# Four lo buffers, two pairs of buffers in turns for the activations, and an earlier last gate piece in layer 0

## The chip, the cores and the metric

The kernel runs on one core of one Trainium2 chip. Its time is the device time of one execution in microseconds (us). The core's engines are TensorE (PE in the profile; its weight loads are PEld), VectorE (DVE), ScalarE (ACT), GpSimd (POOL, almost unused here) and SyncE (SP), which issues the loads of the weights.

## What is computed

One launch computes two transformer blocks of two layers each, on one sequence of 256 tokens with 1024 features, in float32. Cut to what matters:

```python
def first_block(...):                 # layers 0 and 1
    for l in range(DEPTH):
        sh1, sc1, gt1, sh2, sc2, gt2 = split(silu(c) @ w_ada[l] + b_ada[l], 6)
        u = x * (1 + sc1) + sh1
        y = mixer(u, ...)
        x = layer_norm(DN_ALPHA * x + (1 + gt1) * y, ...)
        u = x * (1 + sc2) + sh2
        h = square(relu(u @ w_up[l])) @ w_down[l]
        x = layer_norm(DN_ALPHA * x + (1 + gt2) * h, ...)

def mixer(u, ...):
    q, k, v, glu_in, g_attn, g_conv = split(u @ w_in)
    y_attn = moba_attention(q, k, v) @ w_attn_br
    h = a * sigmoid(g)                # the two halves of glu_in
    h = silu(layer_norm(depthwise_conv31(h) + dw_b, ln_g, ln_b))
    y_conv = h @ w_pw
    return (sigmoid(g_attn) * y_attn + sigmoid(g_conv) * y_conv) @ w_out

def second_block(...):                # layers 2 and 3
    for l in range(DEPTH):
        h = rmsnorm(x, ...)           # three attentions ya, yb, yc from h @ w_in
        gates = sigmoid(h @ w_gate[l] + b_gate[l])
        merged = sum(gates[b] * (y[b] @ w_br[b]))
        x = x + merged @ w_o[l]
        h = rmsnorm(x, ...)
        x = x + (silu(h @ w_ffn_gate[l]) * (h @ w_ffn_up[l])) @ w_ffn_down[l]
    return rmsnorm(x, final_norm_g)
```

## The kernel before

**Weights.** All weights are streamed once, in pieces of 128 x 2048 float32 (1 MB), in the order of a list (`weight_order`). `fetch` (L126 to L141) loads a piece into one of three `raw` buffers by a DMA on SP's queue (L131), ACT casts it to `whi` (L138, in two halves of 128 x 1024, four buffers) and DVE subtracts to get the rest `wlo` (L139, two halves, three buffers). Activations are split in the same way by `split` (L149 to L151: ACT the high part, DVE the low one). A product takes three matmuls: high by high, low weight by high activation, high weight by low activation. So a piece is ready when both halves of its `wlo` are written, and a `wlo` buffer comes free when the last matmul that reads it is done.

**Order.** On PE the instructions stand in the order of the program. DVE, ACT and SP get theirs from a list scheduler when the kernel is built, which also takes the number of buffers into account; each engine then works through its list in order. Small side work (the condition's projection at L374, L419, L421 and L439, attention, convolution) is put between the pieces by `tick`.

**Handovers.** Between a mixer and a feed-forward part, and between two layers, `handover` (L671) orders PE, DVE and ACT by hand. It runs the last matmuls of the output projection (L206 to L208), adds the residual, normalises each of the two halves of 128 tokens (DVE, L761 to L778 for LayerNorm; L841, L845 and L883 for RMS norm; L866 to L877 for the LayerNorm that is followed by an RMS norm), transposes the result on PE (L732), writes the new activation `u` (LayerNorm: DVE L794, ACT L801, DVE L803 and L808; RMS norm: L905, L907) and starts the next projection (L222, L223, L228) before the second half is normalised. There are eight of them: three with LayerNorm, one with both norms (block 1 to block 2), three with RMS norm and the last at the end of the kernel. `later` holds back the splits of pieces that are fetched afterwards until the handover's last instructions; splits of pieces fetched before it may be placed by the scheduler anywhere ahead or inside.

**Buffers of activations.** `u` (high and low, 16 KB a partition) has one buffer, pool `u2`. A pool `s8` of four 8 KB buffers holds `xT` at the start, the two gates `gt` and the merged result `mg` of `mixer1`, and in block 2 `n_`, `kTc`, two of the three `gt` and `mg`.

**Layer 0's mixer.** `mixer1` computes q, k, v and the gates from `w_in`. The depthwise convolution is 30 taps on DVE (L952), spread over the mixer. Its output is transposed on PE by the first `next(cl)` (L967), normalised on DVE (L969, `moments`, L972), transposed back (L332, second `next(cl)`), passed through silu (L982, L983, L985) and split into `hc` (L150, L151), which the convolution's branch, `branch(1, hc, c, merge)`, multiplies by its weights. Around these steps stand the attention's branch in two pieces, `branch(0, y, 0)` and `branch(0, y, 1)`, and the last piece of the gates, `gates(1, [3])`:

```python
        self.finish(conv)
        ...
        next(cl)
        branch(0, y, 0, None)
        next(cl)
        branch(0, y, 1, None)
        gates(1, [3])
        ...
        for c in range(2):
            branch(1, hc, c, merge)
```

**Feed-forward of block 1.** `ffn1` takes the pieces of `w_up` and `w_down` in turns: an up piece (L175, L177), evacuated by ACT (L188) and DVE (L189), squared, split, and multiplied by a down piece (L206 to L208).

Of the kernel before, what the change touches and what calls it, by code (L numbers as in the profile page):

```python
# [9 lines left out]
F32 = mybir.dt.float32  # L10
F32R = mybir.dt.float32r
# [5 lines left out]
P = 128  # L17
D = 1024
S = 256
KT = D // P  # L20
# [44 lines left out]
class Net:  # L65
    def __init__(self, ctx, tc, ins, out, stop=None, dump=None):
        self.tc, self.nc, self.i, self.out = tc, tc.nc, ins, out
        self.stop, self.dumps = stop, dump or {}
        self.uid = 0
        self.pools = {}  # L70
        for name, bufs in (("raw", 3), ("whi", 4), ("wlo", 3), ("s8", 4), ("u2", 1), ("s4", 7), ("b4", 2), ("one", 1), ("sm", 3)):
            self.pool(ctx, name, bufs)
        self.pool(ctx, "ps", 8, space=PSUM)
        self.pool(ctx, "dr", 1, space=bass.MemoryType.DRAM)
        self.queue = weight_order(ins)
        self.ready = []
        self.tracks = []
        self.behind = []
        self.ada = {}
# [268 lines left out]
    def new_u(self):  # L348

        t = self.t("u2", [P, 2, KT, S], F32R)  # L350
        return t[:, 0], t[:, 1], t

    def new_fm(self, n=KT, pool="s8"):
        return self.t(pool, [P, n, S], F32R), self.t(pool, [P, n, S], F32R)
# [175 lines left out]
    def start(self):  # L530


        nc, i = self.nc, self.i
# [8 lines left out]
        a, n = PC["b_ada"]  # L542
        self.par1 = self.t("one", [P, n], tag="par1")
        nc.vector.tensor_scalar(self.par1, self.par[:, a:a + n], 1.0, None, op0=ALU.add)
        u = self.new_u()
        xT = self.t("s8", [P, KT, S])
        A, B = self.ada_cols(0, 1), self.ada_cols(0, 0)
# [3 lines left out]
        a, n = CC["cmask"]  # L551
# [438 lines left out]
    def mixer1(self, l, u, ps):  # L990
        nc, i = self.nc, self.i
        first = l == 0
# [56 lines left out]
        def qkf(h):  # L1049
            r = slice(64 * (h % 2), 64 * (h % 2) + 64)  # L1050
            return qT[r, h // 2, :], kT[r, h // 2, :]
        gt = [self.t("s8", [P, KT, S]) for _ in range(2)]

# [34 lines left out]
        hc = self.new_fm(4, "s4")  # L1088
        cl = self.conv_ln(l, cv, hc)
        next(cl)  # L1090
        branch(0, y, 0, None)
        next(cl)
        branch(0, y, 1, None)
        gates(1, [3])
        self.finish(ada)
        self.dump(f"hc{l}", hc[0].bitcast(F32))
        mg = self.new_fm()

# [110 lines left out]
    def mixer2(self, l, u, ps):  # L1209
# [3 lines left out]
        pcs = [[p for _, p in ps], [p for _, p in self.as_512(u)]]  # L1213
        n_ = self.new_fm()
        mn = self.mla_norm(pcs, gq, n_)
# [63 lines left out]
        qTc = self.t("s8x", [P, 8, S])  # L1279
        kTc = self.t("s8", [P, 8, S])  # L1280
        for src, dst in ((qcs, qTc), (kcs, kTc)):
# [41 lines left out]

        gt = [self.t("s8x" if b == 1 else "s8", [P, KT, S]) for b in range(3)]
        bh = self.small(24, "bgh")
        nc.vector.tensor_scalar(bh, self.par_("b_gate", l * 24, 24), 0.5, None, op0=ALU.mult)
        for b in (2, 0, 1):
            for c in range(4):
                w = self.w()
                for m in range(2):  # L1330
# [4 lines left out]
                    nc.scalar.activation(g, g, AF.Tanh, scale=0.5, bias=bh[:, b * 8 + k:b * 8 + k + 1])  # L1335
        mg = self.new_fm()
        for b in (2, 0, 1):
# [125 lines left out]
def weight_order(i):  # L1463

    o = []
    for l in range(L):
        w = i["w_in_a" if l == 0 else "w_in_b"]
        o += [w[c] for c in range(w.shape[0])]
        last = o.pop()
        o += [i["w_attn_br"][l, c] for c in range(2)] + [last]  # L1470
        for name in ("w_conv_pw", "w_out"):
            o += [i[name][l, c] for c in range(i[name].shape[1])]
        o += [i["w_up"][l, c] for c in range(3)]
        for c in range(3, 19):
            if c < 16:
                o.append(i["w_up"][l, c])
            o.append(i["w_down"][l, c - 3])
# [18 lines left out]
def build(tc, ins, out, stop=None, dump=None):  # L1496
    with ExitStack() as ctx:
# [6 lines left out]
        if stop is None or stop.startswith("2"):  # L1504
            with ExitStack() as c2:
                for name, bufs in (("bias", 3), ("s8x", 1)):
                    net.pool(c2, name, bufs)
                net.block2()
# [149 lines left out]
```

## Time and profile before

| What | Value |
|---|---|
| Runs | 1732.88, 1733.07, 1734.87 us, median 1733.07 |
| Profiled execution | 1733.14 us, of it span of the trace 1731.2 |
| Busy: PE, DVE, ACT | 1661.8, 1281.8, 958.8 us (96, 74, 55%) |
| Share of the chain that ended last | PE 89%, DVE 7%, DMA 2%, ACT 1% |
| Granted TensorE clock, mean | 0.989 of full speed |

The profile is of one execution. PE is busy for nearly the whole span, so time can be taken only out of the stretches in which PE waits, and out of those in which its clock is granted at half (1.2 instead of 2.4 GHz, written 0.50). The views below show where these are: who let PE wait and how long, the chain of work that ended last in order of time, the instructions of one engine in a stretch, and the granted clock in stretches.

### The profile page before, as it was taken

The page shows a single profiled execution, that of the slowest core. Times are in us where ns is not written, and L with a number is a line of the kernel's source. Part 1 is how long each engine was busy: PE and PEld are TensorE (multiplying, and loading weights), DVE is VectorE, ACT ScalarE, POOL GpSimd, SP SyncE. Part 2 cuts the span into 40 slices and gives each one's busy share as a digit, 9 for nine tenths or more (in the row PEclk, how much of TensorE's full clock was granted, in tenths as well). Part 3 has the DMA queues.
Part 4 walks back from the last instruction along what each step waited for, and adds up shares of the span by engine and source line. Part 5 has one row for each costly group of instructions (what it writes and reads, how often), then busy time and mean ns, then how long its engine had stood idle before and what let it go on. Part 6 is the DMA issues. An engine that isn't in the chain of part 4 may idle for free.

```text
span 1731.2 us, 25828 instructions
## 1 busy us (share of the span) xinstructions
PE 1661.8 (96%) x10008; PEld 1436.9 (83%) x10008; DVE 1281.8 (74%) x2497; ACT 958.8 (55%) x1750; POOL 2.6 (0%) x12
## 2 busy tenths in 40 slices
PE   6998999998999999997999999999999999999998
PEld 5887888787888888885988898888889888988887
DVE  7999788578997886557856677766676566876665
ACT  3564375464355375553566754655455677455553
POOL 0000000000000000000000000000000000000000
PEclk9999999999999999998999999999999999999999
DMA  8884568584874466653544444555545444445551
GB/s 337 342 318 173 199 223 316 196 294 176 308 247 182 171 229 233 219 192 140 208 152 150 147 151 179 195 195 195 191 150 203 149 147 146 164 168 198 182 190 72
DMA packets 59974, 347.37 MB, mean 201 GB/s; under 512 B 6558, under 2 KB 10700, under 8 KB 25676
## 3 DMA queue, kind: packets, MB, share of 16 engines
q1 hardware_dynamic: 59852, 345.73, 55.3%
q8 instruction: 78, 1.28, 0.3%
q14 instruction: 44, 0.36, 0.1%
HBM read 344.63 MB, written 2.64 MB: 201 GB/s over the span
## 4 chain that ended last, share of the span: by engine, by line
PE 89%; DVE 7%; DMA 2%; ACT 1%; issue 0%; SPq 0%; DVEq 0%; ACTq 0%
PE ps L175 23%; PE ps L177 12%; PE ps L207 8%; PE ps L206 8%; PE ps L208 8%; PE ps L160 5%; PE ps L161 5%; PE ps L164 4%; PE ps L228 3%; PE ps L222 3%; PE ps L223 2%; DVE wlo L139 2%; PE ps L439 1%; PE ps L332 1%; PE ps L487 1%; PE ps L464 1%
## 5 line engine op out<-in xcount | busy, mean ns | idle before, releaser
L139 DVE TENSOR_TENSOR wlo<-raw,whi 128x1024 fp32r<-128x1024 f32 (+1 forms) x534 | 629.7, 1211 | 206.3 <-PE ps L177 104.0
L138 ACT CAST whi<-raw 128x1024 fp32r<-128x1024 f32 (+1 forms) x534 | 534.1, 1043 | 279.4 <-PE ps L208 80.6
L175 PE MATMUL ps<-u,whi 128*128 128x512 f32 x1728 | 438.9, 396 | 0.0
L175 PEld LDWEIGHTS ps<-u,whi 128*128 128x128 f32 x1728 | 313.9, 188 | 65.3 <-issue 5.7
L206 PE MATMUL ps<-whi,s 128*128 128x512 f32 (+2 forms) x688 | 253.6, 369 | 3.8 <-ACT whi L138 3.8
L207 PE MATMUL ps<-wlo,s 128*128 128x512 f32 (+2 forms) x688 | 253.0, 368 | 0.5 <-DVE wlo L139 0.5
L208 PE MATMUL ps<-whi,s 128*128 128x512 f32 (+2 forms) x688 | 252.3, 367 | 0.0
L177 PEld LDWEIGHTS ps<-u,wlo 128*128 128x128 f32 x1728 | 235.6, 190 | 17.2
L177 PE MATMUL ps<-u,wlo 128*128 128x256 f32 x1728 | 240.7, 282 | 0.0
L206 PEld LDWEIGHTS ps<-whi,s 128*128 128x128 f32 x688 | 130.3, 189 | 23.9 <-ACT whi L138 4.0
L208 PEld LDWEIGHTS ps<-whi,s 128*128 128x128 f32 x688 | 130.0, 189 | 21.0 <-DVE s L151 0.7
L207 PEld LDWEIGHTS ps<-wlo,s 128*128 128x128 f32 x688 | 130.2, 189 | 19.8 <-DVE wlo L139 1.2
L222 PE MATMUL ps<-whi,u 128*128 128x512 f32 x240 | 98.2, 409 | 11.0 <-ACT u L801 10.9
L188 ACT COPY ev<-ps 128x256 f32<-128x256 f32 x136 | 50.2, 369 | 92.1 <-PE ps L177 92.1
L952 DVE SCALAR_TENSOR_TENSOR s<-s,dw,s 128x255 f32<-128x255 f32 (+17 forms) x240 | 96.2, 462 | 0.0
L223 PE MATMUL ps<-wlo,u 128*128 128x512 f32 x240 | 96.0, 400 | 0.0
L160 PE MATMUL ps<-u,whi 128*128 128x256 f32 x352 | 89.4, 292 | 0.2 <-DVE s L941 0.2
L161 PE MATMUL ps<-u,whi 128*128 128x256 f32 x352 | 85.9, 282 | 0.0
L160 PE MATMUL ps<-s,whi 128*128 128x256 f32 x320 | 82.4, 289 | 0.0
L161 PE MATMUL ps<-s,whi 128*128 128x256 f32 x320 | 81.0, 285 | 0.3 <-DVE s L151 0.3
L189 DVE TENSOR_TENSOR ev<-ps,ev 128x256 f32<-128x256 f32 x136 | 56.8, 420 | 28.9 <-ACT ev L188 28.1
L151 DVE TENSOR_TENSOR s<-ev,s 128x256 fp32r<-128x256 f32 (+1 forms) x72 | 39.1, 542 | 48.9 <-PE ps L207 37.7
(263 smaller groups left out, 2123.2 us busy)
## 6 DMA issues: line engine op xcount, KB each, us to landing
raw<-in_w_fgu_dram SPq DMA_DIRECT2D x44, 1024.0 KB, 4.8
raw<-in_w_up_dram SPq DMA_DIRECT2D x32, 1024.0 KB, 5.0
raw<-in_w_down_dram SPq DMA_DIRECT2D x32, 1024.0 KB, 5.6
raw<-in_w_in_dram SPq DMA_DIRECT2D x32, 1024.0 KB, 4.8
ada<-in_w_ada_p_dram SPq DMA_DIRECT2D x48, 512.0 KB, 5.1
raw<-in_w_gate_dram SPq DMA_DIRECT2D x24, 1024.0 KB, 4.8
raw<-in_w_fd_dram SPq DMA_DIRECT2D x22, 1024.0 KB, 4.8
raw<-in_w_in_b_dram SPq DMA_DIRECT2D x18, 1024.0 KB, 6.1
```

Source lines behind the costliest of these rows:

```text
L138: nc.scalar.copy(hi[:, a:b], raw[:, a:b])
L139: nc.vector.tensor_sub(lo[:, a:b], raw[:, a:b], hi[:, a:b].bitcast(F32))
L160: mm(ps, whi[:, b], ahi[:, k, :], start=j == 0, stop=False)
L161: mm(ps, whi[:, b], alo[:, k, :], start=False, stop=False)
L175: mm(p2, whi[:, (blk + k) * P:(blk + k + 1) * P], both[:, :, k, :], start=k == 0, stop=False)
L177: mm(p[:, :S], wlo[:, (blk + k) * P:(blk + k + 1) * P], uhi[:, k, :], start=False, stop=k == KT - 1)
L206: mm(ps, ahi[:, k, tok], whi[:, cols], start=first, stop=False, **grp)
L207: mm(ps, ahi[:, k, tok], wlo[:, cols], start=False, stop=False, **grp)
L208: mm(ps, alo[:, k, tok], whi[:, cols], start=False, stop=last, **grp)
L222: mm(p, ahi[:, k, tok], whi[:, cols], start=k == 0, stop=False)
L223: mm(p, ahi[:, k, tok], wlo[:, cols], start=False, stop=False)
L952: nc.vector.scalar_tensor_tensor(cv[:, ct, d:], hp[:, ct, :S - d], wk, cv[:, ct, d:], op0=ALU.mult, op1=ALU.add)
```

## The change

It has three parts.

1. Pool `wlo` gets four buffers instead of three.
2. To make room, pool `s8` goes. Pool `u2` now holds two buffers of 16 KB by the names `ua` and `ub`. `new_u` takes them in turns; `xT`, `gt`, `mg` and `n_` are halves of one or both. In block 2 `s8x` gets a second buffer, for `kTc`.
3. In layer 0 alone, `gates(1, [3])` is written ahead of the first `next(cl)`, and `weight_order` lists its weight piece ahead of the two pieces of `w_attn_br`. Layer 1 keeps its order.

```diff
-        for name, bufs in (("raw", 3), ("whi", 4), ("wlo", 3), ("s8", 4), ("u2", 1), ("s4", 7), ("b4", 2), ("one", 1), ("sm", 3)):
+        for name, bufs in (("raw", 3), ("whi", 4), ("wlo", 4), ("u2", 1), ("s4", 7), ("b4", 2), ("one", 1), ("sm", 3)):
...
     def new_u(self):
-        t = self.t("u2", [P, 2, KT, S], F32R)
+        self.turn = not self.turn
+        t = self.pair("ua" if self.turn else "ub", F32R)
         return t[:, 0], t[:, 1], t
+    def pair(self, tag, dt=F32):
+        return self.t("u2", [P, 2, KT, S], dt, tag=tag)
...
-        xT = self.t("s8", [P, KT, S])
+        xT = self.pair("ub")[:, 0]
...
-        gt = [self.t("s8", [P, KT, S]) for _ in range(2)]
+        gt = self.pair("ub")
+        gt = [gt[:, b] for b in range(2)]
...
         cl = self.conv_ln(l, cv, hc)
+        if first:
+            gates(1, [3])
         next(cl)
         branch(0, y, 0, None)
         next(cl)
         branch(0, y, 1, None)
-        gates(1, [3])
+        if not first:
+            gates(1, [3])
...
-        mg = self.new_fm()
+        mg = self.pair("ua", F32R)
+        mg = mg[:, 0], mg[:, 1]
...
-        n_ = self.new_fm()
+        n_ = self.pair("ub", F32R)
+        n_ = n_[:, 0], n_[:, 1]
...
-        gt = [self.t("s8x" if b == 1 else "s8", [P, KT, S]) for b in range(3)]
+        gt = self.pair("ub")
+        gt = [gt[:, 0], self.t("s8x", [P, KT, S]), gt[:, 1]]
...
-        o += [i["w_attn_br"][l, c] for c in range(2)] + [last]
+        br = [i["w_attn_br"][l, c] for c in range(2)]
+        o += br + [last] if l else [last] + br
...
-                for name, bufs in (("bias", 3), ("s8x", 1)):
+                for name, bufs in (("bias", 3), ("s8x", 2)):
```

No instruction is added or taken away. The order of the instructions changes at the following places, among others. In the listings a row is line, operation, output, inputs and size; line numbers in the changed kernel are larger (L139 becomes L140, L761 L767, L794 L800, L967 L973, L969 L975), and numbers behind a name count buffers.

DVE in the first handover, before (`ps_2074` holds the projection's result for the second half of the tokens, `ps_2262` the transposed first half; L794 starts the new `u`):

```order
L778 TENSOR_SCALAR x_119<-x_119,mv_2242,r_r_2250 128x512
L761 TENSOR_TENSOR ev_2287<-ps_2074,G_263_1683 128x512
L765 SCALAR_TENSOR_TENSOR x_119<-x_119,ev_2287 128x512
L768 BN_STATS bn_346_2286<-x_119 128x6
L139 TENSOR_TENSOR wlo_2151<-raw_2148,whi_2150 128x1024 x2
L794 TENSOR_SCALAR ev_2284<-ps_2262,pl_a_2161,pl_b_2162 128x128 x2
```

The same place after:

```order
L784 TENSOR_SCALAR x_116<-x_116,mv_2237,r_r_2245 128x512
L767 TENSOR_TENSOR ev_2282<-ps_2069,G_238_1637 128x512
L771 SCALAR_TENSOR_TENSOR x_116<-x_116,ev_2282 128x512
L774 BN_STATS bn_344_2281<-x_116 128x6
L800 TENSOR_SCALAR ev_2279<-ps_2257,pl_a_2156,pl_b_2157 128x128 x2
```

And after, ahead of the handover's first DVE instruction (L767; before, `wlo_2143` stood last ahead of it, and `wlo_2143` of before is `wlo_2138` here, `wlo_2151` is `wlo_2146`):

```order
L152 TENSOR_TENSOR ua_1934<-ub_744,ua_1934 128x512
L140 TENSOR_TENSOR wlo_2138<-raw_2135,whi_2137 128x1024 x2
L140 TENSOR_TENSOR wlo_2146<-raw_2143,whi_2145 128x1024 x2
L767 TENSOR_TENSOR ev_2200<-ps_2067,G_238_1637 128x512
L771 SCALAR_TENSOR_TENSOR x_116<-x_116,ev_2200 128x512
```

The two halves of L139 have moved from inside the handover to the place right ahead of it. The same is found in the next six handovers; the last has none in either kernel.

ACT in the feed-forward of layer 0, before (`ps_3275` and `ps_3302` hold an up piece's result, `whi_3229` is the down piece that PE uses next, `whi_3268` the up piece behind it):

```order
L188 COPY ev_3274<-ps_3275 128x256
L188 COPY ev_3274<-ps_3302 128x256
L1118 ACTIVATE ev_3274<-ev_3274 128x512
L1119 ACTIVATE ev_3274<-ev_3274 128x512
L150 CAST s_517_3323<-ev_3274 128x512
L138 CAST whi_3229<-raw_3227 128x1024 x2
L138 CAST whi_3268<-raw_3266 128x1024 x2
```

After (`whi_3224` is `whi_3229` of before, `whi_3263` is `whi_3268`):

```order
L151 CAST s_484_3122<-ev_3078 128x512
L139 CAST whi_3224<-raw_3222 128x1024 x2
L189 COPY ev_3169<-ps_3170 128x256
L189 COPY ev_3169<-ps_3197 128x256
L1129 ACTIVATE ev_3169<-ev_3169 128x512
L1130 ACTIVATE ev_3169<-ev_3169 128x512
L151 CAST s_499_3218<-ev_3169 128x512
L189 COPY ev_3269<-ps_3270 128x256
L189 COPY ev_3269<-ps_3297 128x256
L1129 ACTIVATE ev_3269<-ev_3269 128x512
L1130 ACTIVATE ev_3269<-ev_3269 128x512
L151 CAST s_515_3318<-ev_3269 128x512
```

The cast of the down piece has moved two up pieces ahead; that of the up piece behind it still follows L151 of `s_515_3318`. DVE's subtractions moved with them: the down piece's stands two up pieces earlier, and that of the up piece behind it (`wlo_3264`) now follows three instructions of side work (L425, L427, L380).

PE in layer 0's mixer, before (`ev_1519` and `ev_1525` are attention's, `s_59_499` the convolution's output, `ps_1670` the attention's branch):

```order
L510 MATMUL ps_1471<-ev_1519,s_57_497 64x128
L510 MATMUL ps_1471<-ev_1525,s_57_497 64x128
L967 MATMUL ps_1612<-con_118,s_59_499 128x128 x4
L967 MATMUL ps_1637<-con_118,s_59_499 128x128 x4
L160 MATMUL ps_1670<-s_102_745,whi_1301 128x256
```

After, the end of the last gate piece (`ps_1612`) and what follows it:

```order
L162 MATMUL ps_1612<-ua_103,whi_1297 128x256
L165 MATMUL ps_1612<-ua_103,wlo_1298 128x256 x8
L445 MATMUL ps_1670<-ada_1642,c_sel_486 32x256 x4
L445 MATMUL ps_1670<-ada_1644,c_sel_486 32x256 x4
L973 MATMUL ps_1686<-con_115,s_59_496 128x128 x4
L973 MATMUL ps_1711<-con_115,s_59_496 128x128 x4
L161 MATMUL ps_1744<-s_102_742,whi_1424 128x256
```

The gate piece now lies between attention's last matmul and the transposes of the convolution's output. DVE behind the convolution, before, from the last tap on:

```order
L952 SCALAR_TENSOR_TENSOR s_59_499<-s_58_498,dw_500,s_59_499 128x226 x2
L139 TENSOR_TENSOR wlo_1665<-raw_1662,whi_1664 128x1024
L969 BN_STATS bn_238_1617<-ps_1612 128x6
L969 BN_STATS bn_249_1642<-ps_1637 128x6
L322 BN_AGGR mv_1619<-bn_238_1617 128x2
L139 TENSOR_TENSOR wlo_1665<-raw_1662,whi_1664 128x1024
L304 TENSOR_SCALAR r_x_1621<-mv_1619 128x1
```

The same place after:

```order
L958 SCALAR_TENSOR_TENSOR s_59_496<-s_58_495,dw_497,s_59_496 128x226 x2
L140 TENSOR_TENSOR wlo_1607<-raw_1604,whi_1606 128x1024 x2
L425 TENSOR_TENSOR G_238_1637<-ps_1638,b_222_1459 128x256
L975 BN_STATS bn_247_1691<-ps_1686 128x6
L427 TENSOR_SCALAR G_238_1637<-G_238_1637 128x256
L323 BN_AGGR mv_1693<-bn_247_1691 128x2
L975 BN_STATS bn_258_1716<-ps_1711 128x6
L305 TENSOR_SCALAR r_x_1695<-mv_1693 128x1
L140 TENSOR_TENSOR wlo_1739<-raw_1736,whi_1738 128x1024
L305 TENSOR_SCALAR r_y_1696<-r_x_1695 128x1
L323 BN_AGGR mv_1718<-bn_258_1716 128x2
L140 TENSOR_TENSOR wlo_1739<-raw_1736,whi_1738 128x1024
```

Four halves of `wlo` and one pair of L425 and L427 now stand ahead of the first normalised half (L972, now L978) where two halves did. From the last tap to the last split of `hc` (L151, now L152) it is seven halves, where it was four.

## Rows read from the trace of the kernel before

**Rows 1.** Waits of PE: line, releaser, us in total, times, longest us.

```profile
PE ps L732 <- DVE s L883: 18.0, 8, 8.3
...
PE ps L222 <- ACT u L801: 10.9, 6, 3.0
PE ps L967 <- DVE s L952: 5.8, 1, 5.8
```

**Rows 2.** The chain that ended last, in order of time: start, us, what.

```profile
210.64 2.36 DVE wlo L139 x2
235.43 1.85 PE ps L175 x8
...
1535.76 2.36 DVE wlo L139 x2
```

**Rows 3.** Timeline of DVE in the first handover: start, us, instruction, idle before it.

```profile
210.64 2.36 DVE L139 TENSOR_TENSOR wlo<-raw,whi 128x1024 fp32r<-128x1024 f32 x2
...
219.02 0.54 DVE L778 TENSOR_SCALAR x<-x,mv,r_r 128x512 f32<-128x512 f32 x1
```

**Rows 4.** Timeline of PE in the first handover.

```profile
214.40 0.50 PE L222 MATMUL ps<-whi,u 128*128 128x512 f32 x1 [3.02 <-ACT u L801]
...
220.67 0.60 PE L732 MATMUL ps<-con,x 128*128 128x128 f32 x4
```

**Rows 5.** Stretches: length, busy by engine, PEclk (granted clock), DMA share, GB/s.

```profile
216.00:217.00 1.00, 1.00 (x4) 0.81 (x3) 0.93 (x4) 0.41 (x1) 0.00 (x0) 0.50 0.95 401
...
411.00:413.00 2.00, 1.97 (x9) 1.63 (x10) 1.99 (x5) 1.97 (x5) 0.00 (x0) 1.00 0.93 352
```

**Rows 6.** Timeline of DVE, then of PE, in the first RMS handover.

```profile
1073.23 2.36 DVE L139 TENSOR_TENSOR wlo<-raw,whi 128x1024 fp32r<-128x1024 f32 x2 [1.25 <-PE ps L207]
...
1080.79 0.30 PE L732 MATMUL ps<-con,s 128*128 128x128 f32 x1 [1.75 <-DVE s L883]
```

**Rows 7.** Timeline of ACT, then of DVE, at the start of the first handover.

```profile
198.11 2.00 ACT L138 CAST whi<-raw 128x1024 fp32r<-128x1024 f32 x2 [3.44 <-PE ps L208]
...
200.79 0.69 DVE L761 TENSOR_TENSOR ev<-ps,G 128x512 f32<-128x512 f32 x1 [0.53 <-PE ps L208]
...
203.66 0.42 DVE L761 TENSOR_TENSOR ev<-ps,G 128x256 f32<-128x256 f32 x1 [0.67 <-PE ps L208]
```

**Rows 8.** Layer 0's feed-forward: timelines of PE, ACT, DVE, and a stretch.

```profile
336.18 0.80 PE L206 MATMUL ps<-whi,s 128*128 128x512 f32 x1 [3.84 <-ACT whi L138]
...
335.08 5.78 ACT L138 CAST whi<-raw 128x1024 fp32r<-128x1024 f32 x6
...
329.90 0.41 DVE L419 TENSOR_TENSOR G<-ps,b 128x256 f32<-128x256 f32 x1
330.35 0.29 DVE L421 TENSOR_SCALAR G<-G 128x256 f32<-128x256 f32 x1
...
338.43 1.28 DVE L374 CUSTOM_DVE_ANT_0 ada<-ada,c_row,par 128x1024 f32<-128x1024 f32 x1
...
338.00:340.00 2.00, 2.00 (x6) 1.54 (x5) 2.00 (x4) 2.00 (x4) 0.00 (x0) 0.50 0.00 0
```

**Rows 9.** Layer 0's mixer: timelines of PE and DVE, and a stretch.

```profile
149.49 1.27 PE L967 MATMUL ps<-con,s 128*128 128x128 f32 x4 [5.81 <-DVE s L952]
...
167.89 0.47 PE L160 MATMUL ps<-u,whi 128*128 128x256 f32 x1
...
175.26 0.47 PE L160 MATMUL ps<-s,whi 128*128 128x256 f32 x1
...
155.63 0.80 DVE L972 TENSOR_SCALAR ev<-ps,mv,r_r 128x512 f32<-128x512 f32 x1
...
169.29 0.69 DVE L151 TENSOR_TENSOR s<-ev,s 128x512 fp32r<-128x512 f32 x1
...
150.00:152.00 2.00, 2.00 (x10) 2.00 (x11) 2.00 (x3) 0.00 (x0) 0.00 (x0) 0.50 0.04 8
```

**Rows 10.** The page's groups: line, engine, operation, count, busy, mean ns, idle before.

```profile
L189 DVE TENSOR_TENSOR ev<-ps,ev 128x256 f32<-128x256 f32 x136 | 56.8, 420 | 28.9 <-ACT ev L188 28.1
```

More of the change, by code (lines that the diff above doesn't have):

```diff
@@ L77, in __init__ @@
         self.tracks = []
+        self.turn = False
         self.behind = []
@@ L348, in new_u, with new_fm @@
     def new_u(self):
-        t = self.t("u2", [P, 2, KT, S], F32R)
+        self.turn = not self.turn
+        t = self.pair("ua" if self.turn else "ub", F32R)
         return t[:, 0], t[:, 1], t
-    def new_fm(self, n=KT, pool="s8"):
+    def pair(self, tag, dt=F32):
+        return self.t("u2", [P, 2, KT, S], dt, tag=tag)
+    def new_fm(self, n, pool):
         return self.t(pool, [P, n, S], F32R), self.t(pool, [P, n, S], F32R)
@@ L1279, in mixer2 @@
         qTc = self.t("s8x", [P, 8, S])
-        kTc = self.t("s8", [P, 8, S])
+        kTc = self.t("s8x", [P, 8, S])
         for src, dst in ((qcs, qTc), (kcs, kTc)):
@@ L1335, in mixer2 @@
                     nc.scalar.activation(g, g, AF.Tanh, scale=0.5, bias=bh[:, b * 8 + k:b * 8 + k + 1])
-        mg = self.new_fm()
+        mg = self.pair("ua", F32R)
+        mg = mg[:, 0], mg[:, 1]
         for b in (2, 0, 1):
```

## Prediction

> **What bounds the kernel now.** PE is busy for 96% of the span (the table), so I read first who lets it wait. In the waits of PE [rows 1] three of the long ones matter here: the transposes of the normalised halves wait for DVE (L732 for L883: 18.0 us in eight waits, the longest 8.3), the first projection of a handover waits for ACT's `u` (L222: 10.9 us in six, the longest 3.0), and in layer 0 the transposes of the convolution's output wait 5.8 us for its last taps (L967). Then I look for what keeps the releaser. In the chain in order of time "DVE wlo L139 x2" stands seven times within a handover, at 210.64, 407.27, 598.25, 783.44, 1073.23, 1261.18 and 1535.76, each 2.35 or 2.36 us (the first and the last are in [rows 2]). The timeline of DVE shows the first of them between the residual work and the step that makes `u` [rows 3]. These two halves belong to a weight piece that nothing in the handover reads. With three `wlo` buffers, two are held by the last pieces of the output projection and one by the next piece, so the split has to wait until one comes free, and that is inside the handover.
>
> **Part 1, the fourth lo buffer: handovers.** In the order of after both halves stand ahead of the handover, seven times. What returns is read from the wait that ends last in each.
>
> First handover. L222 starts at 214.40 after a wait of 3.02 [rows 4]; its input comes from DVE through L794 and ACT, right behind the two halves, so 2.36 come back. The wait shrinks to 0.7. There is more: behind the long wait the clock was granted at 0.50 for three us (one of them in rows 5), half speed, in which up to 1.5 are lost. The second transposes start at 220.67 [rows 4], while `x` was ready at 219.02 + 0.54 = 219.56 [rows 3], so at most 1.1 of that can be regained before DVE is the limit. I take 0.8: 3.2 in all, bounds 2.4 and 3.5.
>
> A row and a rule differ a little here. After the same wait of 3.0 in the second handover the clock stayed at 1.00 (411 to 413 in [rows 5]). The Trainium skill (TensorE: Matmul & The Clock Gate, Part 1, What's actually happening) says that the clock falls to half after an idle stretch and that the window that is watched runs free of the program; by this, equal waits can cost clock in one place and none in another, and the traces agree (0.50 after one, 1.00 after the other). By the rule the 0.8 might stay lost here or turn up elsewhere, and the sum would be 0.8 smaller. That case is a rival below.
>
> Second and third handover: same waits, no clock loss, and DVE carries the chain to the second transposes as well: 2.36 each. Fourth, with both norms: PE waits for DVE throughout (8.3 at its longest [rows 1]), so DVE's 2.35 is the gain. Fifth to seventh (RMS): the second transposes wait 1.75 for L883 (the first of them, at 1080.79, is in [rows 6]), which lies behind the two halves on DVE. This wait goes whole; beyond it PE's own work is the limit, except for a small gap that L905 (also behind the halves) leaves. So between 1.75 and 2.36, and I take 2.0 each. Sum: 3.2 + 4.7 + 2.4 + 6.0 = **16.3**, bounds 14.0 (5.2 for the last three, 2.4 for the first, 0.1 lost in each as below) and 17.7.
>
> What the moved halves now stand in front of: L761, the handover's first DVE step. Their cast still needs a `whi` buffer that PE frees at 198.1 (ACT, 198.11 to 200.11 [rows 7]). The low half follows its cast, so the last ends near 200.11 + 1.2 = 201.3 to 201.5, and L761, at 200.79 before [rows 7], starts 0.6 or 0.7 later. The cover is DVE's idle time of 0.67 ahead of the next L761 at 203.66 [rows 7]. So I cost it at nothing (up to 0.1 each); without that cover it would be 0.7 each.
>
> **Part 1, feed-forward of layer 0.** At 336.18 PE waits 3.84 for a cast of a down piece, which ACT did in a run of six halves from 335.08, after a long time without any [rows 8]. In the order of after this cast and its subtraction stand two up pieces earlier, so the wait goes. Behind it the clock was at half (0.50 in 338 to 340 [rows 8]): from 336.18 to 341 I estimate 4 to 5 us at half speed, which lose about 2.2. Against this stands a new wait. The subtraction of the next up piece (`wlo_3264`) now stands on DVE behind L425, L427 and L380, which are L419, L421 and L374 of before: 0.41 + 0.29 + 1.28 [rows 8]. They start when PE's ones-matmul (L418) is done, right ahead of the up piece; with the first half of the subtraction (1.18) PE's low matmuls can start 3.2 after that, and PE gets there after eight high ones, 1.85 [rows 2]. So PE waits about 1.3. Sum 3.84 + 2.2 - 1.3 = **4.7**; bounds 2.5 (no clock regained) and 6.0 (no new wait). Elsewhere in the order I find no other split with so little room.
>
> **Part 2, the buffers.** Counts and sizes stay. `mg` in `ua` may be written once the last gate piece has read `u`; on PE that piece lies ahead of the branch whose result `mg` holds. The next `u` in `ub` comes after the merge's last read. No queue gets a new wait, cost nothing. If that were wrong the place is the first merge of each mixer.
>
> **Part 3, the earlier gate piece.** It takes PE from 167.89 to 175.26, 7.4 us [rows 9], and fills the wait of 5.81 ahead of L967 at 149.49 [rows 9]. Behind that wait the clock was 0.50 (150 to 152 [rows 9]): 1.0 is lost in these two us, and I estimate as much again for the us on either side, some 1.9. By PE alone, then, 5.81 + 1.9 = 7.7 could come back, the upper bound. But DVE is next. Its last split of `hc` ends at 169.29 + 0.69 = 169.98 [rows 9], and the last tap does not move. In the order of after, seven halves of L140 instead of four stand in between, 3 x 1.18 = 3.5 more. Of the first transposed half (L972, at 155.63 [rows 9]) PE's transposes back will have to wait some 2.5, where PE had its own work before. I take it that one of the three halves falls into time in which DVE waits anyway: `hc` ends near 172.3. The convolution's branch then starts near 172.3 instead of 175.26 [rows 9]: **3.0**. Lower bound 0, if DVE's chain slips by another 3. Its SP loads and casts move with the piece and were early there.
>
> **Sum.** 16.3 + 4.7 + 3.0 = 24.0. The profiled execution took 1733.14, 0.07 above the median of the runs (1733.07), so nothing is corrected: 1733.1 - 24.0 = **1709.1**. Bounds: 14.0 + 2.5 + 0 = 16.5 gives 1716.6; 17.7 + 6.0 + 7.7 = 31.4 gives 1701.7.
>
> **Rivals.**
> 1. *Layer 0's move gives nothing.* DVE's chain from the last tap to `hc` takes all that PE gains. For it: three more halves in that chain, and the taps end when they did. Against: `hc` had 5.3 us of room (169.98 to 175.26), and three halves are 3.5. Time 1733.1 - 21.0 = 1712.1.
> 2. *The moved halves hold up the handover's start.* Decides when the cast ends over 0.1 later than I read it: the cover is 0.67, used to 0.6. If the whole 2.36 is paid ahead of L761 in the three LayerNorm handovers and the fourth, 4 x 2.36 = 9.4 of the gain is lost: 1718.5. Against: PE's release of the buffer at 198.1 doesn't depend on the change.
> 3. *The clock stays low where I have it return*, after the waits that are left in the first handover (0.7) and the feed-forward (1.3): 0.8 + 2.2 lost, 1712.1. Against: the long waits that went before the low clock are gone.
> 4. *The pairs add a wait*, and the change doesn't do what it says: a merge that waits for the last reader of `u` in each of four layers, 6 us each, ends at 1733. Against: the order on PE.
> 5. *Slower.* Earlier splits stand in DVE's in-order list ahead of evacuations of PSUM (L189, 136 of them [rows 10]) and wait there for their cast, so that PE finds no free bank. The idle time ahead of L189 is 28.9 / 136 = 0.21 each [rows 10]; from a new PE wait of 24.0 / 136 = 0.18 each the gain is gone, at 0.25 the time is 1709.1 + 34.0 = 1743.1. Against: the waits of PE name L189 nowhere, so PSUM has had slack.
>
> **How the numbers follow.** Forecast (all three parts within their bounds, 1702 to 1716): 0.58. Rival 1: 0.14, rival 2: 0.12, rival 3: 0.10, rival 4: 0.03, rival 5: 0.03. The first three end within 1709 to 1719, so the range is 1701 to 1719, and 0.06 of the cases and some tails lie outside it. Within 0.2% is about what a measurement of this kernel can tell from no change, 3.5 us: only rival 4 and part of others, 0.04; slower 0.03; faster 0.93.
>
> **What would show it.** In the profile of after: no "DVE wlo x2" of 2.36 within the seven handovers of the chain; L222's successor waits 0.7 instead of 3.0 (the sum of the six near 4, where it was 10.9); the wait of L732's successor for L883's near 10, where it was 18.0; no wait of 3.8 for a cast near 330, and one of about 1.3 for `wlo` instead; the transposes of the convolution's output without a wait, new waits of PE for DVE's L972 and `hc`, 2 to 3 us each. The prediction is wrong if L761's successor starts a us or more later after PE's last matmul of the first half, if PE waits for splits in the feed-forward loops, or if the wait for `hc` is over 5.

## The result and the profile after

| | Before | After |
|---|---|---|
| Median of four runs | 1732.97 us | 1708.53 us (1706.39 to 1710.40) |
| Ratio, 95% interval | | 0.9857 (0.9840 to 0.9874) |
| Profiled execution, span in it | 1733.14, 1731.2 | 1710.40, 1708.3 |

The time fell by 24.4 us; 24.0 were forecast (1709.1). The profiled execution of after is the slowest of its four runs; its span is 22.9 us shorter. The sum is right, but one of its terms is not, and a gain that was not forecast made up for part of it. To see this, the waits of PE in the kernel after (line, releaser, us in total, times, longest):

```profile
PE ps L738 <- DVE s L889: 11.9, 5, 6.1
...
PE ps L223 <- ACT ub L807: 2.6, 4, 0.8
PE ps L424 <- ACT ev L448: 1.9, 1, 1.9
PE ps L161 <- ACT s L151: 1.7, 1, 1.7
PE ps L207 <- ACT whi L139: 1.4, 1, 1.4
PE ps L178 <- DVE wlo L140: 1.3, 1, 1.3
PE ps L223 <- ACT ua L807: 1.1, 2, 0.6
```

Against [rows 1]: the wait for L883 fell from 18.0 to 11.9 (L889 now). The wait for `u` fell from 10.9 to 3.7; it has two rows now, since `u` is called `ua` or `ub`. The wait of 5.8 for the taps is gone. New are L424 (1.9) and L161 (1.7), both in layer 0's mixer, and L178 (1.3) in its feed-forward.

Where the time went is read by setting the same PE instruction of both profiles side by side. Each gain is the growth of the lead since the row above; the first gain counts from the start of the span.

| Place (PE instruction) | Before | After | Lead | Gain |
|---|---|---|---|---|
| Layer 0, convolution's branch starts (L160) | 175.26 | 172.88 | 2.38 | |
| the same branch, when the clock is back (L160) | 178.32 | 177.95 | 0.37 | 0.4 |
| First handover, second transposes (L732) | 220.67 | 216.87 | 3.80 | 3.4 |
| Feed-forward, near its end (L206) | 389.06 | 380.12 | 8.94 | 5.1 |
| Second handover, first projection (L222) | 411.03 | 399.62 | 11.41 | 2.5 |
| Layer 1, condition's projection (L439) | 476.96 | 464.23 | 12.73 | 1.3 |
| Third handover, second transposes (L732) | 607.32 | 592.16 | 15.16 | 2.4 |
| Fourth, behind its second transposes (L223) | 809.17 | 792.58 | 16.59 | 1.4 |
| Fifth (RMS), second transposes | 1080.79 | 1062.09 | 18.70 | 2.1 |
| Sixth | 1268.73 | 1247.93 | 20.80 | 2.1 |
| Seventh | 1543.32 | 1520.43 | 22.89 | 2.1 |
| End of the span | 1731.2 | 1708.3 | 22.9 | 0.0 |

The handovers gave 16.1, the feed-forward 5.1, layer 0's mixer 0.4 (0.3 of which was there already at 45 us, from the start of the kernel), and the condition's projection 1.3: there PE waited 1.1 for a DMA of `ada` before, and no longer does.

**A handover.** DVE in the first handover after (timeline; what the engine waited for stands in brackets):

```profile
198.82 2.36 DVE L140 TENSOR_TENSOR wlo<-raw,whi 128x1024 fp32r<-128x1024 f32 x2 [3.12 <-ACT whi L139]
201.09 0.68 DVE L767 TENSOR_TENSOR ev<-ps,G 128x512 f32<-128x512 f32 x1
...
203.28 0.42 DVE L767 TENSOR_TENSOR ev<-ps,G 128x256 f32<-128x256 f32 x1
```

The two halves wait for their cast and hold L767 up until 201.09. With PE's lead of 0.38 at this point it would have started at 200.41, so it is 0.7 late. But the next L767 comes at 203.28, which is 203.66 [rows 7] less the lead: the idle time of 0.67 has taken all of it. In the third handover, where the lead is 12.73, the same sums give 0.7 and 0.03. PE's first projection in the first handover, and the second transposes in an RMS handover:

```profile
211.54 0.50 PE L223 MATMUL ps<-whi,ub 128*128 128x512 f32 x1 [0.54 <-ACT ub L807]
...
1062.09 0.30 PE L738 MATMUL ps<-con,s 128*128 128x128 f32 x1
```

0.54 for 3.02 [rows 4], and nothing for 1.75 [rows 6]: in the RMS handover PE's own work is the limit now.

**Clock.** Stretches of the kernel after (length, then busy us and instructions of PE, PEld, DVE, ACT, POOL, then the granted clock, DMA share, GB/s):

```profile
162.00:164.00 2.00, 2.00 (x12) 2.00 (x11) 0.88 (x3) 0.85 (x3) 0.00 (x0) 0.50 0.09 33
174.00:176.00 2.00, 2.00 (x13) 2.00 (x13) 2.00 (x3) 0.00 (x0) 0.00 (x0) 0.59 0.44 145
211.00:215.00 4.00, 3.46 (x15) 2.85 (x16) 3.76 (x12) 2.51 (x6) 0.00 (x0) 1.00 0.00 0
328.00:336.00 8.00, 8.00 (x39) 6.64 (x38) 2.46 (x5) 6.05 (x8) 0.00 (x0) 1.00 0.01 2
```

In the first handover (211 to 215) and in the feed-forward (328 to 336) the clock is full, where it was at half [rows 5, 8]. In layer 0's mixer it is at half twice, and PE is busy all the while, with 12 or 13 instructions in 2 us where full clock allows some 19.

**Layer 0's mixer.** Timeline of PE after:

```profile
160.63 1.18 PE L424 MATMUL ps<-ev,ones 128*128 128x256 f32 x2 [1.88 <-ACT ev L448]
161.60 1.91 PE L333 MATMUL ps<-con,ev 128*128 128x128 f32 x8
...
172.88 0.39 PE L161 MATMUL ps<-s,whi 128*128 128x256 f32 x1 [1.69 <-ACT s L151]
173.60 0.39 PE L162 MATMUL ps<-s,whi 128*128 128x256 f32 x1 [0.34 <-DVE s L152]
```

ACT ahead of the first of these waits, and the last split of `hc` on DVE:

```profile
158.31 1.99 ACT L139 CAST whi<-raw 128x1024 fp32r<-128x1024 f32 x2 [7.10 <-PE ps L162]
160.21 0.36 ACT L448 COPY ev<-ps 128x256 f32<-128x256 f32 x1
...
172.86 0.69 DVE L152 TENSOR_TENSOR s<-ev,s 128x512 fp32r<-128x512 f32 x1 [0.59 <-ACT s L151]
```

The gate piece fills the old wait (PE reaches the transposes at 150.31, and the taps are done), but PE then waits 1.88 for a copy that stands behind two weight casts on ACT, and 1.69 and 0.34 for `hc`. Behind each of the two places the clock falls.

### The profile page after: what moved, and what is told of

Its sections match the earlier page's. It is cut to its first block, busy times and chain, and to the rows that moved or that the text cites. A ratio compares the mean times of both kernels' runs of the same rounds, so it can differ in the third digit from the quotient of the medians.

```text
span 1708.3 us, 25825 instructions
## 1 busy us (share of the span) xinstructions
PE 1658.6 (97%) x10008; PEld 1435.9 (84%) x10008; DVE 1276.4 (75%) x2497; ACT 956.6 (56%) x1750; POOL 2.6 (0%) x12
## 4 chain that ended last, share of the span: by engine, by line
PE 90%; DVE 6%; ACT 1%; DMA 1%; issue 1%; SPq 0%; ACTq 0%; DVEq 0%
PE ps L176 23%; PE ps L178 12%; PE ps L208 8%; PE ps L207 8%; PE ps L209 8%; PE ps L161 5%; PE ps L162 5%; PE ps L165 4%; PE ps L223 3%; PE ps L229 3%; PE ps L224 3%; PE ps L333 1%; PE ps L445 1%; PE ps L493 1%; PE ps L470 1%
## 5 line engine op out<-in xcount | busy, mean ns | idle before, releaser
L140 DVE TENSOR_TENSOR wlo<-raw,whi 128x1024 fp32r<-128x1024 f32 (+1 forms) x534 | 631.6, 1212 | 255.8 <-ACT whi L139 252.4
L139 ACT CAST whi<-raw 128x1024 fp32r<-128x1024 f32 (+1 forms) x534 | 535.0, 1043 | 287.4 <-PE ps L209 71.1
L176 PE MATMUL ps<-ub,whi 128*128 128x512 f32 x1088 | 273.2, 393 | 0.0
L176 PEld LDWEIGHTS ps<-ub,whi 128*128 128x128 f32 x1088 | 198.6, 188 | 37.5
L207 PE MATMUL ps<-whi,s 128*128 128x512 f32 (+1 forms) x464 | 174.6, 376 | 0.0
L208 PE MATMUL ps<-wlo,s 128*128 128x512 f32 (+1 forms) x464 | 174.3, 376 | 0.0
L209 PE MATMUL ps<-whi,s 128*128 128x512 f32 (+1 forms) x464 | 174.0, 375 | 0.0
L176 PE MATMUL ps<-ua,whi 128*128 128x512 f32 x640 | 165.7, 401 | 0.0
L178 PEld LDWEIGHTS ps<-ub,wlo 128*128 128x128 f32 x1088 | 148.3, 190 | 12.4 <-DVE wlo L140 1.8
L178 PE MATMUL ps<-ub,wlo 128*128 128x256 f32 x1088 | 151.8, 282 | 1.3 <-DVE wlo L140 1.3
L176 PEld LDWEIGHTS ps<-ua,whi 128*128 128x128 f32 x640 | 115.3, 188 | 27.8 <-issue 5.7
L958 DVE SCALAR_TENSOR_TENSOR s<-s,dw,s 128x255 f32<-128x255 f32 (+14 forms) x240 | 96.3, 462 | 0.0
L178 PEld LDWEIGHTS ps<-ua,wlo 128*128 128x128 f32 x640 | 87.2, 190 | 6.5
L161 PE MATMUL ps<-ua,whi 128*128 128x256 f32 x352 | 89.3, 292 | 0.2 <-DVE s L947 0.2
L178 PE MATMUL ps<-ua,wlo 128*128 128x256 f32 x640 | 89.0, 282 | 0.0
L162 PE MATMUL ps<-ua,whi 128*128 128x256 f32 x352 | 85.9, 282 | 0.0
L161 PE MATMUL ps<-s,whi 128*128 128x256 f32 x320 | 82.6, 289 | 1.7 <-ACT s L151 1.7
```

The costliest lines, as they stand in the source:

```text
L139: nc.scalar.copy(hi[:, a:b], raw[:, a:b])
L140: nc.vector.tensor_sub(lo[:, a:b], raw[:, a:b], hi[:, a:b].bitcast(F32))
L161: mm(ps, whi[:, b], ahi[:, k, :], start=j == 0, stop=False)
L162: mm(ps, whi[:, b], alo[:, k, :], start=False, stop=False)
L176: mm(p2, whi[:, (blk + k) * P:(blk + k + 1) * P], both[:, :, k, :], start=k == 0, stop=False)
L178: mm(p[:, :S], wlo[:, (blk + k) * P:(blk + k + 1) * P], uhi[:, k, :], start=False, stop=k == KT - 1)
```

## The experiments

Ratios are to the kernel before on the same chip. In most of the expectations theory A is that the fourth lo buffer brings the gain and the earlier gate piece is paid for by new waits and clock; the rivals stand beside it.

### The changed kernel again

> The changed kernel once more, beside the others on one chip, as the base that they are compared with. Every theory: a ratio of 0.986 to the kernel before, that is 1708 us where the one before takes 1733.

> The changed kernel in more rounds, as the base of the two others on this chip. Every theory: a ratio near 0.985 to the kernel before.

Measured: 1709.34 us, 0.9847 (0.9824 to 0.9870), and 1707.86, 0.9849 (0.9834 to 0.9863). The result repeats. In both new profiles (span 1706.8) the clock stays full at 162 to 164 and falls only at 173 to 176:

```profile
162.00:164.00 2.00, 2.00 (x20) 2.00 (x18) 1.94 (x6) 1.90 (x5) 0.00 (x0) 1.00 0.20 78
174.00:176.00 2.00, 2.00 (x11) 2.00 (x11) 1.56 (x2) 0.00 (x0) 0.00 (x0) 0.50 0.61 205
```

PE's waits are the same 1.9, 1.7 and 0.3. So one and the same wait of 1.9 took the clock in one execution and not in two others. This is worth 1.6 us, all of the 1.5 between the spans: PE is level with the first profile up to that wait (within 0.1) and 1.6 ahead of it from 165 us on.

### Three lo buffers

```diff
-("wlo", 4)
+("wlo", 3)
```

> The changed kernel with three lo buffers instead of four; pairs and the earlier gate piece stay. Theory A (the fourth lo buffer brings the gain): 1731 to 1735 us, with the two halves of 2.36 us inside seven handovers again and a wait for a cast of near 3.8 in layer 0's feed-forward. Theory B (the pairs of activation buffers loosen the order by themselves and bring a part): 1712 to 1728 us.

Measured: 1730.79 us, 0.9967 (0.9956 to 0.9977). Of the chain that ended last, the rows within the handovers, and then PE's waits, of this kernel:

```profile
207.55 2.36 DVE wlo L140 x2
404.24 2.36 DVE wlo L140 x2
596.01 2.36 DVE wlo L140 x2
781.21 2.35 DVE wlo L140 x2
1070.99 2.36 DVE wlo L140 x2
1258.94 2.36 DVE wlo L140 x2
1533.52 2.36 DVE wlo L140 x2
```

```profile
PE ps L738 <- DVE s L889: 18.0, 8, 8.3
...
PE ps L223 <- ACT ub L807: 7.3, 4, 3.0
PE ps L207 <- ACT whi L139: 4.9, 2, 3.8
```

All seven are back, with the waits of before (18.0, 3.0 each, 3.8). The fourth buffer is worth 1730.8 - 1709.3 = 21.5 us; 21.0 were forecast for it (16.3 + 4.7). Theory A.

The clock shows something here too. The first handover's wait is 3.0 as before, but now the clock stays; the second's is 3.02 as before, and now the clock falls:

```profile
213.00:215.00 2.00, 2.00 (x10) 1.66 (x9) 1.75 (x8) 0.32 (x1) 0.00 (x0) 1.00 0.55 229
...
409.00:411.00 2.00, 2.00 (x6) 1.57 (x5) 1.86 (x7) 0.98 (x3) 0.00 (x0) 0.54 0.88 373
```

In the kernel before it was the other way round [rows 5]. In the kernel of the next section, which has three lo buffers too, the clock falls in the first handover and in the third:

```profile
214.00:218.00 4.00, 4.00 (x12) 3.09 (x12) 3.68 (x14) 1.70 (x5) 0.00 (x0) 0.62 0.56 233
...
601.00:604.00 3.00, 3.00 (x9) 2.33 (x8) 2.79 (x10) 1.39 (x4) 0.00 (x0) 0.50 0.71 300
```

So of the nine such waits in three profiles four were followed by half clock; which one is not set by the wait. In the ten profiles with four lo buffers PE waits for `u` 0.8 us at most, and in none of them does the clock fall in these three handovers.

### The earlier gate piece alone, and everything but it

The kernel before with the third part alone, `gates(1, [3])` and its weight piece ahead in layer 0:

> The kernel before with the third part alone: the earlier gate piece and its place in the list of weights; buffers as before. Theory A (pairs of activation buffers cost and bring nothing): the same as with pairs and three lo buffers, a ratio near 0.997 to the kernel before, 1727 to 1731 us, and PE's long waits at the same places. Theory B (the pairs cost or bring something): over 2 us away from that.

Measured: 1730.70 us, 0.9974 (0.9960 to 0.9989). With the pairs and three lo buffers it was 0.9967, so the pairs bring and cost nothing that shows: theory A. The move alone took 3.1 us off the medians (1733.79 to 1730.70), clear of nothing by the interval. In its profile the clock stays full in the whole mixer (172 to 178 below), the waits ahead of the convolution's branch are 0.7 and 0.6, and PE gains 3.9 us on the kernel before between 130 and 190 us:

```profile
172.00:178.00 6.00, 4.67 (x35) 4.07 (x34) 5.05 (x11) 2.51 (x3) 0.00 (x0) 1.00 0.75 300
```

The changed kernel without the move:

```diff
-        if first:
-            gates(1, [3])
         next(cl)
...
-        if not first:
-            gates(1, [3])
+        gates(1, [3])
...
-        o += br + [last] if l else [last] + br
+        o += br + [last]
```

> The change without its third part: layer 0's last gate piece stands behind branch(0, y, 1) again; buffers as changed. Theory A (the earlier gate piece gains 7.9 us at its place and gives nearly all of it back, in PE's new waits for ACT and DVE and in two stretches at half clock): 1708.5 us, within 1.5 of the changed kernel, with PE's wait of 5.8 for the last taps back. Theory B (the move is worth the 3.0 us that were forecast): 1711.5 us.

> The changed kernel without the earlier gate piece once more, in more rounds, to size the third part. Theory A (the move gives back what it gains when the clock falls twice behind it, and keeps about 2 when it falls once or not): 0 to 2 us above the changed kernel. Theory B (worth the 3.0 that were forecast): 3 us or more above it.

Measured: 1711.25 us, 0.9859 (0.9842 to 0.9877), beside 1709.34 for the changed kernel; then 1709.26, 0.9855 (0.9838 to 0.9871), beside 1707.86. The wait is back:

```profile
PE ps L973 <- DVE s L958: 5.8, 1, 5.8
```

So with four lo buffers the move is worth 1.9 and 1.4 us by the medians. The first lies between the two theories, the second fits theory A. The intervals overlap, so it is not told from nothing by these runs alone; the 3.0 of the forecast is not reached in either. By the profiles (PE's gain on the kernel before between 130 and 190 us) it is worth 0.1 with two falls of the clock behind it and 1.7 with one.

### Filling the wait ahead of the convolution's branch

```diff
+        if first:
+            p = self.ps().rearrange("p (a t) -> p a t", a=2)
+            for _ in range(8):
+                nc.tensor.matmul(p, self.ready[0][0][:, :P], u[2][:, :, 0, :], start=True, stop=True)
         for c in range(2):
             branch(1, hc, c, merge)
```

> The changed kernel with eight extra 128x512 matmuls in layer 0, whose result nobody reads, right ahead of the convolution's branch: 8 x 0.23 = 1.8 us of work in a place where PE waits 2.0 us. Theory A (the wait ahead of the branch takes the clock): the branch still starts near 172.9, no stretch at 0.50 follows from 173 to 178, and the branch's first 24 matmuls take some 3.3 instead of 5.1 us, so 1.0 to 1.8 us less from there on. Theory B (the clock falls for what lay earlier, or the extra matmuls only push the branch back): the stretch at 0.50 stays, or the branch starts later by what the clock gives.

Measured: a single run, 1708.54 us. The timeline of PE, and the stretches:

```profile
171.60 2.19 PE L1116 MATMUL ps<-ua,whi 128*128 128x512 f32 x8
173.64 0.38 PE L161 MATMUL ps<-s,whi 128*128 128x256 f32 x1
174.37 0.39 PE L162 MATMUL ps<-s,whi 128*128 128x256 f32 x1 [0.34 <-DVE s L152]
```

```profile
174.00:176.00 2.00, 1.66 (x14) 1.63 (x14) 2.00 (x4) 0.00 (x0) 0.00 (x0) 1.00 0.70 250
176.00:178.00 2.00, 2.00 (x19) 2.00 (x18) 2.00 (x3) 0.00 (x0) 0.00 (x0) 1.00 0.57 127
```

The extra work fits in the wait; the branch starts as late as PE's general lag in this execution makes it (2.4 us at 163 already, 2.0 of it from before 130), and the clock stays at 1.00. Of this lag behind the changed kernel's second profile PE makes good 1.5 us between 173 and 177. This fits theory A, that the wait takes the clock, and not what lies earlier. One execution can't show it, since equal waits left the clock alone in other executions; for it stands that the clock fell at this place in all three profiles of the changed kernel, and not in the last kernel below, which has six extra matmuls there.

### Holding the splits back

DVE's chain from the last tap to `hc` holds seven halves of `wlo`. Here the splits of the convolution's two pieces and of the next are issued only after `z`, and after the last split of `hc`, with the kernel's own `later`:

```diff
-        next(cl)
+        held = next(cl)          # conv_ln yields the second L978
+        if first:
+            self.behind = held
         branch(0, y, 0, None)
-        next(cl)
+        held = next(cl)          # conv_ln yields the last split of hc
+        if first:
+            self.behind = held
         branch(0, y, 1, None)
```

> The changed kernel, and in layer 0 the splits of the first weight piece of the convolution's branch are issued only behind the second normalised half (L978), those of its second piece and of the next behind the last split of hc (L152). Five halves of the seven then stand elsewhere. Theory A (DVE's chain from the last tap to hc is the limit behind the earlier gate piece, and its waits cost the clock): hc is ready near 169 instead of 172.9, PE waits under 1 us between the transposes and the convolution's branch, the clock stays at 1.00 from 150 to 180, and the time is 4 to 6 us below the changed kernel, 1702.5 to 1704.5 us. Theory B (another limit is right behind, such as the held splits, which come late for PE): within 1.5 us of the changed kernel.

> The kernel with held splits once more, in more rounds. Theory A: 2 to 3 us below the changed kernel, a ratio of 0.983 to 0.985 to the kernel before, no stretch at half clock in layer 0. Theory B: level with the changed kernel, 0.985 to 0.987.

Measured: 1707.35 us, 0.9840 (0.9814 to 0.9866), beside 1709.34; then 1706.02, 0.9822 (0.9803 to 0.9842). The chain is shorter:

```profile
169.83 0.38 PE L161 MATMUL ps<-s,whi 128*128 128x256 f32 x1 [0.93 <-ACT s L151]
170.85 0.38 PE L162 MATMUL ps<-s,whi 128*128 128x256 f32 x1 [0.64 <-DVE s L152]
```

The branch's first two matmuls start at 169.83 and 170.85, where the changed kernel's second profile (0.3 ahead of this one up to 159) has 171.28 and 172.00: `hc` is ready 1.2 to 1.5 us earlier, and not near 169 as expected. Waits of 0.9 (L424), 0.9 and 0.6 are left. In the first profile no clock is lost in layer 0's mixer, and PE gains 2.9 us there on the changed kernel's second profile; in the second it falls at 174, after these short waits, and PE gains 1.4 us on the changed kernel's third:

```profile
174.00:176.00 2.00, 2.00 (x12) 2.00 (x11) 2.00 (x4) 0.00 (x0) 0.00 (x0) 0.50 0.33 47
```

So theory A holds for the chain in direction, but not in size, and my belief that waits under 1 us are safe for the clock was wrong. The medians fell by 2.0 us beside the changed kernel on the same chip, and the intervals of both series overlap with those of the changed kernel (0.9824 to 0.9870, 0.9834 to 0.9863): the gain is read from the profiles and not from the runs.

### Extra matmuls in the handover with both norms

PE still waits 6.1 and 4.7 to 4.9 us there, and the clock is at half behind both. On top of the held splits:

```diff
             ps = [net.ps() for _ in range(2)]
+            for _ in range(warm):    # 22 ahead of the first, 17 ahead of the second transposes
+                hi = (net.ready or [net.last])[0][0]
+                self.nc.tensor.matmul(ps[0], hi[:, :P], hi[:, :512], start=True, stop=True)
```

> The kernel with held splits, and in the handover with both norms 22 and 17 extra 128x512 matmuls, whose result nobody reads, ahead of the first and the second transposes, where PE waits 6.1 and 4.9 us for DVE: 5.0 and 3.9 us of work. Theory A (these waits take the clock, and the two stretches at 0.50 behind them cost 3.9 us, of which the first 1.6 only lengthen the next wait): no stretch at 0.50 in this handover and 2.3 us less than with held splits alone. Theory B (DVE and ACT are the limit in the whole handover, also behind the second transposes): the clock stays at 1.00, and the time stays within 1 us.

Measured: 1704.80 us, 0.9822 (0.9801 to 0.9844), beside 1706.02 for the held splits. Timeline of PE, then a stretch with these matmuls and one without (held splits alone, the same place):

```profile
769.95 5.18 PE L739 MATMUL ps<-whi 128*128 128x512 f32 x22
776.14 1.09 PE L743 MATMUL ps<-con,s 128*128 128x128 f32 x8 [1.02 <-DVE s L894]
...
788.33 1.09 PE L743 MATMUL ps<-con,s 128*128 128x128 f32 x8 [2.09 <-DVE s L894]
...
790.00:792.00 2.00, 2.00 (x10) 1.66 (x9) 1.80 (x5) 2.00 (x4) 0.00 (x0) 1.00 1.01 330
```

```profile
785.00:787.00 2.00, 2.00 (x7) 1.52 (x6) 1.25 (x4) 1.95 (x6) 0.31 (x1) 0.50 0.94 307
```

The clock stays full, and from the first transposes to behind the second PE gains 2.2 us on the first profile of the held splits and 2.4 on the second (2.3 expected). All eleven profiles without these matmuls, that of the kernel before included, have the clock at half behind both waits; this one and that of the next section have it at neither. The medians differ by only 1.2, within their spread, and this profiled execution was already 3.9 us behind the first of the held splits at 65 us: the profiles show the place and what it gives there, and the medians don't settle the size. Layer 0's mixer is the same as with the held splits alone, and here too the clock falls behind its short waits (0.57 in the mean of 175 to 179).

### All of it

> Held splits, extra matmuls in the handover with both norms, and six extra 128x512 matmuls (1.4 us) ahead of the convolution's branch in layer 0, where PE still waits 1.5 us. Theory A (waits take the clock): no stretch at 0.50 between 60 us and the end of the last handover, and 4 to 5 us below the changed kernel, near 0.982. Theory B (the extra matmuls only take the place of waits): level with held splits alone, 2 us below the changed kernel.

Measured: 1704.45 us (1703.22 to 1705.18), 0.9828 (0.9813 to 0.9843), beside 1707.86 for the changed kernel: 3.4 us less. Layer 0's stretch and the granted clock:

```profile
170.00:174.00 4.00, 3.54 (x30) 3.54 (x30) 4.00 (x6) 0.33 (x1) 0.00 (x0) 1.00 0.62 156
174.00:178.00 4.00, 4.00 (x35) 4.00 (x34) 4.00 (x6) 0.42 (x1) 0.00 (x0) 1.00 0.89 350
```

No stretch at half clock is left between 44 and 1690 us. Of all kernels here this has the lowest median; its interval overlaps that of the changed kernel slightly, so the size of the gain is less sure than its place. The 3.4 lie between the two theories, and beside the kernel before on its own chip the held splits alone stood at 0.9822, no worse: the runs don't tell the two apart, and theory A is borne out for the clock alone.

## Why the prediction was right, step by step

**What bounds the kernel.** Right: the two halves in each handover were what PE waited for. With the fourth buffer they are gone from there, with three they are back, seven times.

**Handovers, 16.3.** Measured 16.1: 3.4 in the first (3.2), 2.5 and 2.4 in the next two (2.36 each), 1.4 in the fourth (2.35), and 2.1 in each of the RMS ones (2.0 each). The fourth fell short for a reason that was not in the sum: its first transposes came 2.1 earlier, and 0.7 was lost again from the second ones on, which ran at half clock where before they began at full clock (before, then after):

```profile
804.61 1.25 PE L732 MATMUL ps<-con,s 128*128 128x128 f32 x8 [3.44 <-DVE s L883]
...
787.32 1.94 PE L738 MATMUL ps<-con,s 128*128 128x128 f32 x8 [4.74 <-DVE s L889]
```

The cover was read rightly: the moved halves hold up L767 by 0.7, and the idle time behind takes all of it but 0.0 to 0.03. Rival 2 did not occur.

**First handover's clock, 0.8 of its 3.2.** The clock stayed full. The Trainium skill (TensorE: Matmul & The Clock Gate, Part 1, What's actually happening) says that the window that is watched runs free of the program. The traces agree in more than I used: equal waits take the clock in one place and not in another, and which one it is changes from profile to profile. So it is luck of the profile that I read that a fall stood in the first handover. It is not luck that a fall goes: with three lo buffers three profiles have four falls in these three handovers, with four buffers ten profiles have none.

**Feed-forward, 4.7.** Measured 5.1. The wait of 3.8 is gone, and the clock is full: it is at half behind that wait in all three profiles with three lo buffers, and in none of the ten with four. The new wait for `wlo` is 1.34, forecast 1.3:

```profile
337.68 0.50 PE L178 MATMUL ps<-ub,wlo 128*128 128x256 f32 x2 [1.34 <-DVE wlo L140]
```

**The buffers, 0.** Right, by the pair of runs with three lo buffers.

**The earlier gate piece, 3.0.** This term is the step that failed. Its DVE part was nearly right: `hc` was forecast for 172.3. In the first profile its last split ended at 173.55 (172.86 + 0.69), in the two later ones, where the clock stays full at 162, at 171.95 and 171.87. But I added the new waits (2.5 at the transposes back, some more at `hc`) as if they cost their own length only. The clock fell behind both of them. The first fall took 1.6 us, as the later profiles show. The second took 1.6 of the lead of 1.96 that was left when the branch's second matmul started (175.56 before, 173.60 after). I had named the clock as a rival only at the places where it was low before, and behind the waits that are left there, not at those of the mixer where the change makes PE wait. The profile kept 0.4, in which 0.3 came from the start of the kernel; later runs put the term at 1.4 to 1.9. It was mis-sized by some 1 to 3 us. Without the two falls it would be some 3.3, an estimate from 0.1 + 1.6 + 1.6; the one profile of the move without a fall, with three lo buffers and shorter waits, shows 3.9. One detail was unseen: the wait at L424 is for a copy on ACT, which stands behind two weight casts (158.31), and not for L978.

**What was not in the sum.** 1.3 us in layer 1, where a load of `ada` no longer makes PE wait. The wait is there with three lo buffers and pairs as well (1.2 us in two waits), and with four buffers it is missing or 0.3; but it is missing too in the profile of the move alone, with three buffers. So the cause stays open.

With this and the 0.4 of the feed-forward the total came out right by partly cancelling errors: -0.2 for the handovers, +0.4, -2.6 for the gate piece and +1.3 on 24.0 for the profiled span (22.9). That the median of the runs fell by 24.4, so near to the forecast, is in part luck.

## What to carry to other kernels

A weight buffer that comes free only inside a serial stretch puts its refill into that stretch: look there for work whose result nobody in the stretch reads, and count buffers back from the place where it should stand. Work moved into a wait of PE shortens that wait only until the next engine in the chain is late; cost the new waits with the half clock that may follow them (1.6 us for each of the two falls here), also where they last only one or two microseconds. Where a wait can't be removed, matmuls whose result nobody reads can hold the clock, provided they end before the wait does: in the handover with both norms the clock stayed full in both profiles that have them, and fell in all eleven without.

## What was not expected of the hardware

- The same wait takes the clock in one execution and not in another: 1.9 us at L424 in the changed kernel (0.50 at 162 to 164 in one profile, 1.00 in two others), 3.0 us in the first two handovers (0.50 in the first and 1.00 in the second with the kernel before, the reverse with three lo buffers and pairs).
- Waits of 0.9, 0.9 and 0.6 us within 12 us were followed by 0.50 in one of two profiles of the kernel with held splits, and waits of 1.1, 0.9 and 0.6 in that with extra matmuls, whose mixer is the same. What PE did in between was not the cause that one could read off: it ran the same instructions in all three.
- Profiles differ by up to 4 us within the first 65 us, before any of the places at issue, while the weights' first loads arrive: by 1.5 between two of the held splits, and by 3.9 between the first of these and the kernel with extra matmuls, which differs from it only further on. A difference of 1 or 2 us between two profiles has to be read from there on.
